# Expert stage 1 of a two-block transformer kernel: gate steps of four tokens, gates stored in pairs, and a lookup by predicated copies

## The chip, the cores and the metric

The kernel runs on one core of one Trainium2 chip. The metric is the device time of one execution in microseconds (us), as the median of several runs. A core has five engines that work side by side, each through its own queue in order: TensorE (PE; PEld is its weight load), VectorE (DVE), ScalarE (ACT), GpSimd (POOL) and SyncE (SP), which issues most of the DMAs. TensorE writes to PSUM, a small memory of eight banks; VectorE and ScalarE can read PSUM, GpSimd cannot.

## The reference

One attention block with a product-key expert layer (PEER), then a second block of two mixers. The change is in the expert layer, for 512 tokens of width 1024, eight heads and 16384 = 128 x 128 experts:

```python
q = (hx @ w_q).reshape(TOKEN_BLOCK, PEER_HEADS, 2, PEER_HALF)
s = einsum('nhpd,hpkd->nhpk', q, sub_keys)               # 2 x 128 scores a head
top_s, top_i = lax.top_k(s, PEER_TOPK)                   # 16 of each half
cand = top_s[:, :, 0, :, None] + top_s[:, :, 1, None, :]
best_s, best_p = lax.top_k(cand.reshape(..., 256), PEER_TOPK)
i1 = take_along_axis(top_i[:, :, 0], best_p // PEER_TOPK)
i2 = take_along_axis(top_i[:, :, 1], best_p % PEER_TOPK)
expert = i1 * N_KEYS + i2                                # 8 x 16 experts a token
gate = softmax(best_s)
act = gelu(einsum('nd,ned->ne', hx, u[expert]))
return einsum('ne,ned->nd', gate * act, v[expert])
```

## The kernel before

The 512 tokens are four tiles of 128. Tile 0 gathers its experts' rows of `u` and `v` from memory and takes row dots (`gathered`, L713). For tiles 1 to 3 (384 tokens) the layer is computed over all experts, in 128 blocks of 128 experts: activations of every token with every expert, times a gate matrix that is zero where a token did not choose an expert.

Expert stage 1 is the loop at L731 over the first SPILL = 88 blocks. A block (`experts_in`, L694) loads 512 KB of `u`, splits it into a high part on ScalarE (L690) and a low part on GpSimd (L691), multiplies it with the tokens in 24 matmuls into one PSUM buffer of the tag `acc` (four buffers), and takes the gelu on ScalarE into `av` (L703), which a DMA stores in A_d (L736). Stage 2 (L803) does the other 40 blocks with `experts_out`, reads back A_d and the gates, multiplies them (L754), and adds up the output.

Between the blocks of stage 1 a hand-made plan (L679 to L685) places other work. A plan entry has a block number; all entries that are due are emitted ahead of that block.

`route(t)` finds the experts of tile t in five steps, spread over ROUTE_AT[t]. Each of the first four does four heads of one half: four or eight matmuls of the queries q2T with the sub-keys skT into a PSUM buffer of the tag `lg` (two buffers; L570), then max, index and replace on VectorE (L576 to L580). q2T[0] holds heads 0 to 3 (steps one and two), q2T[1] the others (steps three and four). The fifth step sums candidates (`cand`, L584, L587), picks 16 of them (L595 to L599), and looks up which key each stands for: the place in the list is split by shifts into two numbers (L602 to L615), and for each half a one-hot compare over 16 places (L624), a product with the indices (L627) and a tree of adds (L629, L630) give `ii`. Then the softmax of the gates.

`slot_major(t)` transposes `ii` and the gates into `eT` through a PSUM buffer of the tag `tp` (two buffers). `gate_matrix(g)` makes the gates of 16 tokens in four steps of four tokens in a row: VectorE compares `eT` with 0..127 for both halves at once into `oh` (L661), ScalarE scales the second half by the gate (L666), TensorE multiplies the two one-hots into a `tp` buffer (L667), and ScalarE writes the four 128 x 128 results into `stage` (L668), which a DMA stores in G_d (L669). `stage` and q2T have the tag "stage" and share its two buffers (L553, L657). GATES_AT places these entries.

The instructions of an engine are not run in the order of the text: the framework orders them by a list schedule with the text's order as priority, and gives a tile its buffer when one is free. Only the transfers marked so keep the order of the text.

Of the kernel before, what the change touches and what calls it, by code (L numbers as in the profile page):

```python
# [10 lines left out]
FT = mybir.dt.float32  # L11
# [12 lines left out]
OT = 8  # L24
# [6 lines left out]
ROUTE_AT = ((0, 12), (12, 25), (25, 44), (44, 63))  # L31
GATES_AT = ((27, 49), (49, 67), (67, 85))
# [59 lines left out]
def block_kernel(ctx: ExitStack, tc: tile.TileContext, A, out):  # L92
# [428 lines left out]
    for j in range(2):  # L521
# [11 lines left out]
    G_d = dram.tile([HG, P, P, GT], FT, name="G_d")  # L533
# [24 lines left out]
    NC1, NC2 = 4 * TOPK, (TOPK - 4) * 4  # L558
    NCD = NC1 + NC2

    def route(t, found):
# [21 lines left out]
        cand = rw.tile([P, PH, NCD], FT, name="cand")  # L583
# [3 lines left out]
        nc.vector.tensor_add(cand[:, :, NC1:NCD].rearrange("p h (a b) -> p h a b", b=4),  # L587
# [21 lines left out]
        late = rw.tile([P, NSLOT], BF, name="late")
        nc.vector.tensor_scalar(late, df[:, 0], 4.0, None, op0=OP.is_ge)  # L610
        abf = rw.tile([P, 2, NSLOT], BF, name="abf")
        nc.vector.scalar_tensor_tensor(df[:, 2], df[:, 2], -12.0, df[:, 0], op0=OP.add, op1=OP.subtract)
        nc.vector.tensor_sub(df[:, 3], df[:, 3], df[:, 1])
        nc.vector.tensor_mul(df[:, 2:4], df[:, 2:4], late[:, None, :].to_broadcast([P, 2, NSLOT]))
        nc.vector.tensor_add(abf, df[:, 0:2], df[:, 2:4])  # L615
        ii = rw.tile([P, 2, NSLOT], FT, name="ii")
        for hf in range(2):
            eq = rw.tile([P, TOPK, NSLOT], BF, name="eq", tag="oh", bufs=4)
            eqs = eq.rearrange("p j (g s) -> p j g s", s=OT)

            tif = rw.tile([P, TOPK, PH, TOPK], BF, name="tif")
            nc.scalar.activation(tif, ti[:, hf].rearrange("p h j -> p j h")[:, :, :, None]
                                 .to_broadcast([P, TOPK, PH, TOPK]), AF.Copy)
            nc.vector.tensor_tensor(eqs, iota_t[:, :, None, :].to_broadcast([P, TOPK, NSLOT // OT, OT]),  # L624
                                    abf[:, hf].rearrange("p (g s) -> p g s", s=OT)[:, None]
                                    .to_broadcast([P, TOPK, NSLOT // OT, OT]), op=OP.is_equal)
            nc.vector.tensor_mul(eq, eq, tif.rearrange("p j h s -> p j (h s)"))  # L627
            for n in (8, 4, 2):
                nc.vector.tensor_add(eq[:, 0:n], eq[:, 0:n], eq[:, n:2 * n])  # L629
            nc.vector.tensor_add(ii[:, hf], eq[:, 0], eq[:, 1])  # L630
# [12 lines left out]
    eT = rz.tile([P, 3, TG], FT, name="eT")  # L643
    found = {}

    def slot_major(t):
# [6 lines left out]
        nc.scalar.activation(eT[:, :, (t - 1) * P:t * P], p[:, 0:3], AF.Copy)  # L653

    def gate_matrix(g):

        stage = rz.tile([P, P, GT], FT, name="stage", tag="stage", bufs=2)  # L657
        for t0 in range(0, GT, 4):
            c = slice(g * GT + t0, g * GT + t0 + 4)
            oh = rw.tile([P, 2, 4, P], FT, name="oh", tag="oh", bufs=4)  # L660
            nc.vector.tensor_tensor(oh, iota_f[:, None, None, :].to_broadcast([P, 2, 4, P]),  # L661
                                    eT[:, 0:2, c, None].to_broadcast([P, 2, 4, P]), op=OP.is_equal)
            p = ps.tile([P, 4, P], FT, name="tp", tag="tp")
            for i in range(4):
                at = g * GT + t0 + i
# [532 lines left out]
```

## Time and profile before

| what | us |
|---|---|
| median of three runs | 2403.86 (2402.47 to 2408.37) |
| the profiled execution, of which the rows are | 2402.58 |
| its span in the trace | 2400.8 |
| TensorE busy in the span | 2255.2 (94%) |
| VectorE, ScalarE, GpSimd busy | 1695.4, 1138.6, 1073.5 |
| expert stage 1, from the first block's split to the second stage's first outputs | about 406 to 985 |

A row of a view names a line of the kernel, the engine, the operation, and which tile is made from which. Busy time is what an engine worked; the idle time in front of an instruction is put down to what ended it. The granted clock (PEclk) is 1.00 at 2.4 GHz and 0.50 at 1.2 GHz; a number between is a mean over a stretch.

### The profile page before, as it was taken

How to read it: one execution, taken by the hardware profiler on the slowest of the kernel's cores; microseconds unless marked ns; L12 is line 12 of the kernel's file. 1: busy time of each engine (PE TensorE's matmuls, PEld its weight loads, DVE VectorE, ACT ScalarE, POOL GpSimd, SP SyncE). 2: the span in 40 equal slices, each digit the busy share in tenths (PEclk: the TensorE clock that was granted, in tenths of full speed). 3: DMA queues.
4: the chain of work that ended last, by engine and by line, in shares of the span. 5: the costliest groups of instructions: out<-in, count | busy, mean ns of one | idle time of the engine just before them, and what ended most of it. 6: DMA issues, size and time to landing. Idle time of an engine off the chain costs nothing.

```text
span 2400.8 us, 32593 instructions
## 1 busy us (share of the span) xinstructions
PE 2255.2 (94%) x11610; PEld 1930.8 (80%) x11610; DVE 1695.4 (71%) x2982; ACT 1138.6 (47%) x2093; POOL 1073.5 (45%) x643
## 2 busy tenths in 40 slices
PE   6989999996998989899999999999899899999998
PEld 5767778996988889799998788888788788867676
DVE  8698445499778777588888888888655445247755
ACT  3644423433467979533333333333455444367742
POOL 4840034565755654388876665656211302212200
PEclk9999999998999999999999999999999999999999
DMA  7456123465766676799998999998311222312121
GB/s 273 143 183 189 62 80 106 150 211 179 246 225 239 242 249 230 262 346 339 333 332 312 341 339 324 327 337 303 116 36 36 71 100 63 112 40 65 32 74 67
DMA packets 205570, 463.04 MB, mean 193 GB/s; under 512 B 17664, under 2 KB 98016, under 8 KB 202336
## 3 DMA queue, kind: packets, MB, share of 16 engines
q1 hardware_dynamic: 168544, 326.72, 41.1%
q0 software_dynamic: 36864, 134.23, 15.3%
q8 instruction: 92, 1.51, 0.3%
q14 instruction: 70, 0.57, 0.1%
HBM read 415.26 MB, written 44.58 MB: 192 GB/s over the span
## 4 chain that ended last, share of the span: by engine, by line
PE 64%; DVE 16%; issue 7%; DMA 6%; ACT 5%; POOL 3%; SPq 0%; DVEq 0%; POOLq 0%; ACTq 0%
PE acc L153 14%; PE acc L154 14%; PE acc L155 14%; PE lg L153 2%; PE lg L154 2%; PE lg L155 2%; PE tp L154 2%; PE tp L153 2%; PE tp L155 2%; PE lg L1095 2%; DMA g<-in_peer_u_dram,idx 2%; DVE oh L661 1%; PE tp L667 1%; DVE g L717 1%; DVE wada L267 1%
## 5 line engine op out<-in xcount | busy, mean ns | idle before, releaser
L691 POOL TENSOR_TENSOR wlo<-wraw,whi 128x1024 fp32r<-128x1024 f32 x172 | 453.8, 2640 | 430.7 <-ACT whi L690 424.4
L690 ACT ACTIVATE whi<-wraw 128x1024 fp32r<-128x1024 f32 x256 | 269.1, 1053 | 221.1 <-PE lg L154 61.4
L153 PE MATMUL acc<-fm,whi 128*128 128x384 f32 (+2 forms) x932 | 329.0, 355 | 7.0 <-ACT av L703 5.1
L154 PE MATMUL acc<-fm,whi 128*128 128x384 f32 (+2 forms) x932 | 323.3, 348 | 0.0
L155 PE MATMUL acc<-fm,wlo 128*128 128x384 f32 (+2 forms) x932 | 321.6, 347 | 1.3 <-POOL wlo L691 1.3
L717 DVE CUSTOM_DVE_ANT_0 g<-g,h20y 128x1024 f32<-128x1024 f32 x128 | 199.0, 1559 | 85.6 <-DMA g<-in_peer_u_dram,idx 85.2
L149 POOL TENSOR_TENSOR wlo<-wraw,whi 128x1024 fp32r<-128x1024 f32 (+4 forms) x56 | 124.4, 2232 | 288.4 <-ACT whi L148 283.5
L757 ACT ACTIVATE wh<-w 128x384 fp32r<-128x384 f32 x128 | 67.0, 524 | 331.9 <-DVE w L754 277.3
L148 ACT ACTIVATE whi<-wraw 128x1024 fp32r<-128x1024 f32 (+5 forms) x142 | 138.1, 980 | 158.6 <-PE acc L155 83.4
L154 PE MATMUL acc<-wlo,wh 128*128 128x512 f32 x512 | 203.0, 397 | 5.1 <-POOL wlo L691 5.0
L728 DVE SCALAR_TENSOR_TENSOR h20y<-g,act,h20y 128x1024 f32<-128x1024 f32 x127 | 189.7, 1494 | 20.3 <-DMA g<-in_peer_v_dram,idx 19.9
L155 PE MATMUL acc<-whi,wl 128*128 128x512 f32 x512 | 201.8, 395 | 0.4 <-DVE wl L758 0.4
L153 PE MATMUL acc<-whi,fm 128*128 128x512 f32 (+3 forms) x496 | 189.7, 387 | 3.6 <-ACT fm L139 2.4
L153 PEld LDWEIGHTS acc<-fm,whi 128*128 128x128 f32 x932 | 176.9, 191 | 19.0 <-ACT av L703 5.4
L709 POOL DMA_INDIRECT g<-in_peer_u_dram,idx x128 | 178.3, 1393 | 29.8 <-issue 16.4
L155 PE MATMUL acc<-whi,fm 128*128 128x512 f32 (+3 forms) x496 | 188.0, 385 | 0.0
L154 PE MATMUL acc<-wlo,fm 128*128 128x512 f32 (+3 forms) x496 | 187.9, 381 | 0.0
L154 PEld LDWEIGHTS acc<-fm,whi 128*128 128x128 f32 x932 | 177.3, 190 | 9.5 <-issue 2.2
L155 PEld LDWEIGHTS acc<-fm,wlo 128*128 128x128 f32 x932 | 177.0, 190 | 9.0 <-POOL wlo L691 1.8
L709 POOL DMA_INDIRECT g<-in_peer_v_dram,idx x128 | 167.2, 1307 | 33.9 <-issue 19.6
L153 PE MATMUL acc<-whi,wh 128*128 128x512 f32 x512 | 182.1, 395 | 0.0
L149 DVE TENSOR_TENSOR wlo<-wraw,whi 128x1024 fp32r<-128x1024 f32 (+3 forms) x86 | 102.3, 1196 | 88.3 <-ACT whi L148 84.6
(356 smaller groups left out, 5415.1 us busy)
## 6 DMA issues: line engine op xcount, KB each, us to landing
wraw<-in_uT_dram SPq DMA_DIRECT2D x128, 512.0 KB
wraw<-in_peer_v_dram SPq DMA_DIRECT2D x128, 512.0 KB
wada<-in_w_adaT_dram SPq DMA_DIRECT2D x48, 512.0 KB
G_d<-stage SPq DMA_DIRECT2D x24, 1024.0 KB
gm<-G_d SPq DMA_DIRECT2D x64, 384.0 KB
A_d<-av SPq DMA_DIRECT2D x88, 192.0 KB
am<-A_d SPq DMA_DIRECT2D x88, 192.0 KB
wraw<-in_w_in_dram SPq DMA_DIRECT2D x24, 512.0 KB
```

Source lines behind the costliest of these rows:

```text
L148: nc.scalar.activation(hi[:, :nk, :n], raw[:, :nk, :n], AF.Copy)
L149: eng.tensor_sub(lo[:, :nk, :n], raw[:, :nk, :n], hi[:, :nk, :n].bitcast(FT))
L153: nc.tensor.matmul(o, lh, rh, start=first, stop=False)
L154: nc.tensor.matmul(o, lh, rl, start=False, stop=False)
L155: nc.tensor.matmul(o, ll, rh, start=False, stop=last)
L690: nc.scalar.activation(hi, raw, AF.Copy)
L691: eng.tensor_sub(lo, raw, hi.bitcast(FT))
L709: tc.keep_in_program_order(nc.gpsimd.indirect_dma_start(out=g, out_offset=None, in_=src, in_offset=bass.IndirectOffsetOnAxis(ap=idx0[:, s: ...
L717: nc.vector.tensor_tensor_reduce(out=g, in0=g, in1=h20, scale=1.0, scalar=0.0, op0=OP.mult, op1=OP.add, accum_out=act0[:, i:i + 1])
L728: nc.vector.scalar_tensor_tensor(y, g, act0[:, s:s + 1], y, op0=OP.mult, op1=OP.add)
L757: nc.scalar.activation(wh, w, AF.Copy)
L1095: nc.tensor.matmul(lg, q[:, t * P:(t + 1) * P], k, start=True, stop=True)
```

## The change

- The gates of a tile are planned in 32 steps of four tokens, one entry each, where there were eight of 16 tokens; a step's result goes into a PSUM buffer of the tag `acc` and no longer `tp`.
- `eT` is not copied to SBUF: the compares read the transposed indices from the `tp` buffer in PSUM. Only the gates are copied (`gT`).
- `stage` and G_d hold pairs of neighbouring key numbers beside each other, [64, 16 tokens, 2] for [128, 16 tokens]; the reader in stage 2 takes every second element.
- The one-hot lookup is replaced by a binary one: the place is cut into four bits, and predicated copies halve a list of 16 until one is left. ScalarE fills the first list and copies the result.
- `cand` has 16 more places between its parts, filled with the lowest number by GpSimd in every route, so that a place splits by bits alone.
- The sub-keys are stored twice, each time with zeros in the other half's rows, and L570 multiplies over 128 rows.
- ROUTE_AT and GATES_AT are moved a little, and tile 0's 60 row dots of this stage are spread over blocks 24 to 87 instead of 13 to 87.

```diff
-ROUTE_AT = ((0, 12), (12, 25), (25, 44), (44, 63))
-GATES_AT = ((27, 49), (49, 67), (67, 85))
+ROUTE_AT = ((0, 11), (11, 23), (23, 43), (43, 62))
+GATES_AT = ((24, 45), (45, 65), (65, 85))
...
-    skT = rz.tile([P, PH, N_KEYS], FT, name="skT")
-    dma(skT, A["subkeysT"])
+    skT = rz.tile([P, PH, 2, N_KEYS], FT, name="skT")
+    for a in range(2):
+        own, other = slice(a * 64, (a + 1) * 64), slice((1 - a) * 64, (2 - a) * 64)
+        nc.gpsimd.memset(skT[other, :, a], 0.0)
+        dma(skT[own, :, a], A["subkeysT"][own])
...
-                    nc.tensor.matmul(lg[:, h * P:(h + 1) * P], q2T[h0 // 4][b0:b0 + 64, h, t * P:(t + 1) * P],
-                                     skT[b0:b0 + 64, h0 + h], start=True, stop=True)
+                    nc.tensor.matmul(lg[:, h * P:(h + 1) * P], q2T[h0 // 4][:, h, t * P:(t + 1) * P],
+                                     skT[:, h0 + h, hf], start=True, stop=True)
...
+        nc.gpsimd.memset(cand[:, :, NC1:NC2], MARK)
...
+        nc.vector.tensor_scalar(ab[:, 0], bpf, 4, 3, **shift_and)
+        nc.vector.tensor_scalar(ab[:, 1], bpf, 15, None, op0=OP.bitwise_and)
+        nc.vector.tensor_scalar(late[:, 0], bpf, 2, 15, **shift_and)
+        nc.vector.tensor_scalar(late[:, 1], bpf, 3, None, op0=OP.bitwise_and)
+        nc.vector.tensor_scalar(far, bpf, 64, None, op0=OP.bitwise_and)
+        nc.vector.copy_predicated(ab, far[:, None, :].to_broadcast([P, 2, NSLOT]), late)
+        bits = rw.tile([P, 4, 2, NSLOT], U32, name="bits")
+        for n in range(4):
+            nc.vector.tensor_scalar(bits[:, n], ab, 1 << n, None, op0=OP.bitwise_and)
...
+            eq = rw.tile([P, 8, NSLOT], FT, name="eq", tag="oh", bufs=4)
+            eqh = eq.rearrange("p j (h s) -> p j h s", h=PH)
+            nc.scalar.activation(eqh, tif[:, hf, 0:8, :, None].to_broadcast([P, 8, PH, TOPK]), AF.Copy)
+            nc.vector.copy_predicated(eqh, bits[:, 3, hf]...,  tif[:, hf, 8:16, :, None]...)
+            for n in (4, 2, 1):
+                nc.vector.copy_predicated(eq[:, 0:n], bits[:, n.bit_length() - 1, hf]..., eq[:, n:2 * n])
+            nc.scalar.activation(ii[:, hf], eq[:, 0], AF.Copy)
...
-        nc.scalar.activation(eT[:, :, (t - 1) * P:t * P], p[:, 0:3], AF.Copy)
+        nc.scalar.activation(gT[:, (t - 1) * P:t * P], p[:, 2], AF.Copy)
+        eT[t - 1] = p[:, 0:2]
...
+    def gate_matrix(q):
+        g, t0 = q * 4 // GT, q * 4 % GT
+        if t0 == 0:
+            stages[g] = rz.tile([P, P // 2, GT, 2], FT, name="stage", tag="stage", bufs=2)
+        e = eT[q * 4 // P][:, :, q * 4 % P:q * 4 % P + 4, None]
+        oh = rw.tile([P, 2, 4, P], FT, name="oh", tag="oh", bufs=4)
+        nc.vector.tensor_tensor(oh, iota_f[:, None, None, :].to_broadcast([P, 2, 4, P]),
+                                e.to_broadcast([P, 2, 4, P]), op=OP.is_equal)
+        p = ps.tile([P, 4, P], FT, name="gp", tag="acc", bufs=4)
+        for i in range(4):
+            nc.scalar.activation(oh[:, 1, i], oh[:, 1, i], AF.Copy, scale=gT[:, q * 4 + i:q * 4 + i + 1])
+            nc.tensor.matmul(p[:, i], oh[:, 0, i], oh[:, 1, i], start=True, stop=True)
+        nc.scalar.activation(stages[g][:, :, t0:t0 + 4], p.rearrange("p i (u w) -> p u i w", w=2), AF.Copy)
+        if t0 + 4 == GT:
+            dma(G_d[g], stages.pop(g))
...
-    turn, first_turn = 0, int(ROUTE_AT[0][1]) + 1
+    turn, first_turn = 0, int(ROUTE_AT[1][1]) + 1
```

## Rows read from the trace of the kernel before

**Rows 1.** The page's slices of 60 us: TensorE busy in tenths.
```profile
PE   6989999996998989899999999999899899999998
```
**Rows 2.** Stage 1 in stretches: length, busy us (instructions) of each engine, clock, DMA.
```profile
core 0: us, PE busy (x) PEld busy (x) DVE busy (x) ACT busy (x) POOL busy (x), PEclk, DMA share, GB/s
...
550.00:600.00 50.00, 33.09 (x174) 31.88 (x175) 48.89 (x111) 22.47 (x45) 27.73 (x14) 0.80 0.53 178
...
700.00:750.00 50.00, 42.04 (x257) 40.39 (x256) 38.45 (x84) 33.62 (x63) 25.19 (x12) 0.93 0.61 217
750.00:800.00 50.00, 43.62 (x278) 42.66 (x279) 47.46 (x114) 42.95 (x93) 30.74 (x13) 0.97 0.63 215
800.00:850.00 50.00, 48.40 (x319) 47.01 (x319) 35.74 (x33) 44.52 (x91) 29.89 (x14) 1.00 0.75 265
850.00:900.00 50.00, 43.68 (x271) 42.18 (x270) 36.48 (x33) 38.10 (x83) 30.02 (x14) 0.97 0.71 243
...
950.00:985.00 35.00, 22.30 (x144) 20.40 (x143) 19.13 (x20) 30.46 (x68) 6.22 (x4) 0.90 0.62 236
sum 579.00, PE 518.22 PEld 498.84 DVE 432.47 ACT 360.85 POOL 321.44; mean PE 43.18 PEld 41.57 DVE 36.04 ACT 30.07 POOL 26.79
```
**Rows 3.** Waits of TensorE, 406 to 990: us in total, times, longest.
```profile
PE tp L667 <- ACT stage L668: 20.0, 19, 2.5
PE tp L650 <- DVE ii L630: 15.5, 1, 15.5
PE tp L667 <- ACT oh L666: 10.4, 4, 5.2
PE lg L153 <- ACT am L703: 5.6, 1, 5.6
PE acc L153 <- ACT av L703: 5.1, 1, 5.1
```
**Rows 4.** Timeline, TensorE and ScalarE: start us, us, engine, instruction.
```profile
587.30 0.27 PE L667 MATMUL tp<-oh 128*128 128x128 f32 x1
...
665.85 1.16 PE L570 MATMUL lg<-skT,q2T 64*128 64x128 f32 x8
...
667.16 1.07 ACT L668 ACTIVATE stage<-tp 128x512 f32<-128x512 f32 x1
```
**Rows 5.** Timeline, VectorE: first and last operation of one route step.
```profile
445.21 0.30 DVE L576 MAX8 ts<-lg 128x8 f32<-128x128 f32 x1 [38.56 <-PE lg L570]
...
450.04 0.28 DVE L580 FIND_INDEX8 ti<-ts,s 128x8 uint32<-128x128 f32 x1
```
**Rows 6.** VectorE on `eq`, on `df` (busy, count); two adds, 406 to 990 (busy, mean).
```profile
406.00:990.00 584.00, 51.46 (x48) 0.96 0.65 218
...
406.00:990.00 584.00, 14.69 (x24) 0.96 0.65 218
...
L629 DVE TENSOR_TENSOR eq<-eq 128x256 bf16<-128x256 bf16 x8 | 14.4, 1797 | 0.0
...
L629 DVE TENSOR_TENSOR eq<-eq 128x1024 bf16<-128x1024 bf16 x8 | 6.9, 863 | 0.0
```
**Rows 7.** VectorE's compare (also min/median/max ns) and row dots, 406 to 990.
```profile
L661 DVE TENSOR_TENSOR oh<-iota_f,eT 128x1024 f32<-128x1024 f32 x96 | 140.4, 1501 | 11.3 <-ACT stage L668 9.6 <-PE tp L667 1.3 <-ACT oh L666 0.3
...
L661 DVE TENSOR_TENSOR oh<-iota_f,eT x96: 1199/1218/3434, 581.1 to 972.3; 128x1024 f32<-128x1024 f32 x96
...
L717 DVE CUSTOM_DVE_ANT_0 g<-g,h20y 128x1024 f32<-128x1024 f32 x63 | 104.9, 1666 | 61.4 <-DMA g<-in_peer_u_dram,idx 61.1 <-issue 0.4
```
**Rows 8.** ScalarE from PSUM, 512 elements: into `stage`, and in runs.
```profile
L668 ACT ACTIVATE stage<-tp 128x512 f32<-128x512 f32 x96 | 94.9, 1069 | 7.9 <-DMA G_d<-stage 6.2 <-PE tp L667 1.7
...
L139 ACT ACTIVATE fm<-tp 128x512 fp32r<-128x512 f32 x48 | 27.3, 595 | 49.8 <-PE tp L137 49.7
```
**Rows 9.** VectorE's max over PSUM and over SBUF, 406 to 990.
```profile
L576 DVE MAX8 ts<-lg 128x8 f32<-128x128 f32 x56 | 16.3, 290 | 49.3 <-PE lg L570 49.3
...
L579 DVE MAX8 ts<-s 128x8 f32<-128x128 f32 x56 | 15.6, 278 | 0.0
```
**Rows 10.** The product with `gm` in stage 2: min/median/max ns.
```profile
L754 DVE TENSOR_TENSOR w<-am,gm x128: 543/552/3284, 992.2 to 1669.3; 128x384 f32<-128x384 f32 x128
```

More of the change, by code (lines that the diff above doesn't have):

```diff
@@ L532, in block_kernel @@
     HG = TG // GT
-    G_d = dram.tile([HG, P, P, GT], FT, name="G_d")
+    G_d = dram.tile([HG, P, P // 2, GT, 2], FT, name="G_d")
     A_d = dram.tile([P, P, TG], FT, name="A_d")
@@ L556, in block_kernel @@
     linear_fm(A["w_peer_q"][0], 8, 512, 512, h2T, NT, lambda m, p: nc.scalar.activation(q2T[1][:, m], p, AF.Copy))
-    NC1, NC2 = 4 * TOPK, (TOPK - 4) * 4
-    NCD = NC1 + NC2
+    NC1, NC2, NCD = 4 * TOPK, 5 * TOPK, 8 * TOPK
+    cand = rz.tile([P, PH, NCD], FT, name="cand")
     def route(t, found):
@@ L609, in route @@
[L609 to L615, printed above, removed]
+        ab = rw.tile([P, 2, NSLOT], U32, name="ab")
@@ new lines, in route @@
+        late = rw.tile([P, 2, NSLOT], U32, name="late")
+        far = rw.tile([P, NSLOT], U32, name="far")
+        shift_and = dict(op0=OP.logical_shift_right, op1=OP.bitwise_and)
+        nc.vector.tensor_scalar(ab[:, 0], bpf, 4, 3, **shift_and)
[3 more added lines that the diff above has]
+        nc.vector.tensor_scalar(far, bpf, 64, None, op0=OP.bitwise_and)
@@ L616, in route @@
+        nc.vector.copy_predicated(ab, far[:, None, :].to_broadcast([P, 2, NSLOT]), late)
+        bits = rw.tile([P, 4, 2, NSLOT], U32, name="bits")
+        for n in range(4):
+            nc.vector.tensor_scalar(bits[:, n], ab, 1 << n, None, op0=OP.bitwise_and)
+        tif = rw.tile([P, 2, TOPK, PH], FT, name="tif")
+        nc.scalar.activation(tif, ti.rearrange("p f h j -> p f j h"), AF.Copy)
         ii = rw.tile([P, 2, NSLOT], FT, name="ii")
         for hf in range(2):
-            eq = rw.tile([P, TOPK, NSLOT], BF, name="eq", tag="oh", bufs=4)
@@ L627, in route @@
[L627 to L630, printed above, removed]
+            eq = rw.tile([P, 8, NSLOT], FT, name="eq", tag="oh", bufs=4)
+            eqh = eq.rearrange("p j (h s) -> p j h s", h=PH)
+            nc.scalar.activation(eqh, tif[:, hf, 0:8, :, None].to_broadcast([P, 8, PH, TOPK]), AF.Copy)
+            nc.vector.copy_predicated(eqh, bits[:, 3, hf].rearrange("p (h s) -> p h s", h=PH)[:, None]
+                                      .to_broadcast([P, 8, PH, TOPK]),
+                                      tif[:, hf, 8:16, :, None].to_broadcast([P, 8, PH, TOPK]))
@@ L631, in route @@
+            for n in (4, 2, 1):
+                nc.vector.copy_predicated(eq[:, 0:n], bits[:, n.bit_length() - 1, hf][:, None]
+                                          .to_broadcast([P, n, NSLOT]), eq[:, n:2 * n])
+            nc.scalar.activation(ii[:, hf], eq[:, 0], AF.Copy)
         ge = rw.tile([P, PH, TOPK], FT, name="ge")
@@ L640, in route @@
         yield
-    eT = rz.tile([P, 3, TG], FT, name="eT")
+    eT = {}
+    gT = rz.tile([P, TG], FT, name="gT")
     found = {}
@@ L652, in slot_major @@
         nc.tensor.transpose(p[:, 2], gt, ident)
-        nc.scalar.activation(eT[:, :, (t - 1) * P:t * P], p[:, 0:3], AF.Copy)
[L655 to L665, printed above, removed]
-                nc.scalar.activation(oh[:, 1, i], oh[:, 1, i], AF.Copy, scale=eT[:, 2, at:at + 1])
-                nc.tensor.matmul(p[:, i], oh[:, 0, i], oh[:, 1, i], start=True, stop=True)
-            nc.scalar.activation(stage[:, :, t0:t0 + 4].rearrange("p i t -> p t i"), p, AF.Copy)
-        dma(G_d[g], stage)
+        nc.scalar.activation(gT[:, (t - 1) * P:t * P], p[:, 2], AF.Copy)
+        eT[t - 1] = p[:, 0:2]
+    stages = {}
+    def gate_matrix(q):
[13 more added lines that the diff above has]
+            dma(G_d[g], stages.pop(g))
     def first_indices():
@@ L683, in block_kernel @@
         plan.append((a, lambda t=t: slot_major(t)))
-        plan += [(at, lambda g=g: gate_matrix(g)) for g, at in enumerate(spread(P // GT, a, b), (t - 1) * P // GT)]
+        plan += [(at, lambda q=q: gate_matrix(q)) for q, at in enumerate(spread(P // 4, a, b), (t - 1) * P // 4)]
     plan.sort(key=lambda step: step[0])
@@ L778, in fetch_gates @@
             if part == 0:
-                gts[b] = dz.tile([P, HG, 8, GT], FT, name="gm")
+                gts[b] = dz.tile([P, HG, 4, GT, 2], FT, name="gm")
             c = slice(part * HG // 4, (part + 1) * HG // 4)
-            paced(gts[b][:, c], G_d[c, :, b:b + 8].rearrange("g p i t -> p g i t"))
+            paced(gts[b][:, c], G_d[c, :, b // 2:b // 2 + 4].rearrange("g p u t w -> p g u t w"))
     def fetch(n):
```

24 lines of the change are left out of this document (2 added, 22 removed).

## The prediction

> **What bounds the kernel now.** I read the page's slices of 60 us first [rows 1]: TensorE is busy nearly everywhere. What the change touches, expert stage 1, lies in slices 7 to 17, and there stand a 6 in slice 10 and an 8 in 13, 15 and 17. So I asked for that stage in 50 us stretches [rows 2]. It runs from about 406 to 985 us. Over these 579 us TensorE was busy 518.2, so 60.8 us were idle; and the granted clock fell to 0.80, 0.93, 0.97, 0.97 and 0.90 in five stretches, which is 0.20 x 50 + 0.07 x 50 + 0.03 x 50 + 0.03 x 50 + 0.10 x 35 = 20.0 us of full-speed time. TensorE's matmuls of the stage are not altered by the diff, so 60.8 + 20.0 = 80.8 us is all that it can win there.
>
> Then the waits of TensorE in the stage [rows 3]. Two kinds stand out. The first is VectorE falling behind: a single wait of 15.5 us for the looked-up indices `ii` of tile 1 and one of 5.1 us for an accumulator that ScalarE could not empty; VectorE was busy 48.9 of the 50 us around them [rows 2], and the clock fell to 0.80 in the same stretch. The second is the gate matrices: 20.0 us waiting for ScalarE's evacuation into `stage` and 10.4 us for its scaling of `oh`, in 23 pieces, because four steps of four tokens are emitted in a row behind one plan entry, while only two PSUM buffers of the tag `tp` take their results. The 5.6 us at the end belong to the tail, where the last gate steps have no expert block left beside them.
>
> One more thing must be seen, for it decides the forecast [rows 4]. The gate steps of tile 1 are planned from block 27, and their first matmuls do run at 587.30 us. But the first evacuation starts at 667.16 us, 80 us later, right behind the eight matmuls of L570 at 665.85. These are the second step of route(3), the last readers of q2T[0]. q2T and `stage` share the tag "stage" with two buffers: no gate tile can be written until route(3) has read q2T[0]. In those 80 us two finished gate results sat in the two `tp` buffers. That cost TensorE nothing, since the experts use the tag `acc`.
>
> **The change, part by part.**
>
> Lookups. What touches `eq` and `df`, the one-hot lookup and the arithmetic on its indices, took 51.5 + 14.7 = 66 us of VectorE over four tiles [rows 6]. The 256-element add in it took 1797 ns, twice the 1024-element one (863), so what makes these operations long is being held up, not their size. New are, per tile, nine predicated copies (one over 256, and for each half 1024, 512, 256, 128 elements) and nine short bit operations in place of five. No predicated copy is in this trace. From below I scale the shortest compare, 1199 ns for 1024 elements [rows 7]: (256 + 2 x 1920) / 1024 x 1.2 = 4.8 us, rounded up to 5.5 for the fixed part of the short ones, and 2.5 for the bit operations: 8 us a tile. From above each copy is held as that 256-element add was, about 1.5 us more: 22 us a tile. I take 12, nearer the lower end since fewer operations wait on each other; that saves 66 - 48 = 18 us of VectorE (bounds: 34 saved, 22 lost). ScalarE loses eight 2048-wide broadcasts and gains eight 1024-wide ones and some small copies, even.
> By the Trainium skill, "SBUF — State Buffer", section "Who interferes with whom", a VectorE instruction with two SBUF inputs contends with a GpSimd instruction that reads SBUF. By it the predicated copies, with list and bits both in SBUF, are exposed like the adds, which agrees with the 1797 ns [rows 6]; with every one held the lookups would cost 22 us more than now in place of 18 less, and VectorE would be late again where it was late for `ii`.
>
> Indices out of PSUM. 96 compares of 1501 ns mean, 140.4 us, with a median of 1218 and a longest of 3434 [rows 7]. The second operand moves from SBUF to PSUM. The nearest rows are the max over `lg` (PSUM), 290 ns, and over `s2` (SBUF), 278 ns [rows 9]: 12 ns more, 1.2 us over 96. If the hold-ups go as well, up to 0.28 x 96 = 27 us fall away. I take 15 us of VectorE saved, bounds 1 lost and 27 saved.
>
> Pairs. The evacuation takes 1069 ns for 512 elements that it writes 64 bytes apart [rows 8]; the same size written in runs takes 595 ns. Now eight elements lie together, but PSUM is read two by two. No row shows such a read: bounds 0.60 and 1.07 us; I take 0.7, near the run-wise row, 96 x 0.37 = 35 us of ScalarE. Behind it, the product with `gm` reads every second element; its shortest runs take 543 ns for 384 elements [rows 10]. Doubled, it would add 0.4 us x 128 to VectorE in stage 2; I take nothing, and keep 10 us of loss in the range.
>
> Four-token steps. 96 steps spread singly over blocks 24 to 85: a step's scalings and evacuation on ScalarE now lie beside a block of experts instead of beside three other steps. That should take most of the 20.0 + 10.4 us of waits, and the tail's 5.6, since the last step is planned at block 84. The stretch 800:850, where gates already alternate with blocks, shows what is left: 1.6 us idle in 50 at full clock [rows 2].
>
> Padded sub-keys: the same 128 columns per matmul, nothing on TensorE; one more DMA and two GpSimd fills before the stage, four fills of `cand` in it (128 elements a partition each), and candidates 128 wide instead of 112: about 3 us of VectorE in all. GpSimd is busy 321 of 579 us [rows 2], so its fills hide; were they not hidden they would cost some 5 us.
>
> Row dots from block 24 instead of 13: the same 60 of 1666 ns [rows 7], so tiles 0 and 1 are routed without them, which takes some ten dots, 17 us, out of the stretch in which VectorE was full. In exchange 0.95 instead of 0.82 of them per block later. I let the 15.5 and 5.1 us waits go for that and the lighter lookups.
>
> What is late next: the gate results now take the tag `acc`, four buffers, which the experts need too. Each holds its buffer until its evacuation, and that waits for q2T[0] as in [rows 4]. From block 24 four results can be ready within some four blocks; then all four buffers are held, and behind them in TensorE's order every expert block waits. TensorE is then free for nothing but the `lg` matmuls of the routes, so routes 2 and 3 are pulled forward until q2T[0] is read. With two `lg` buffers that takes three steps of route(2) on VectorE. One step takes 445.21 to 450.32, 5.1 us [rows 5]. So 3 x 5.1 = 15.3, plus four compares of 1.2 and some five dots of 1.2 (their length when not held up, as the compare's) that come before them, 4.8 + 6: 26 us of hold. For the second `stage` buffer (q2T[1]) one more short hold, 4 us, between nothing and one step.
>
> The sum: 80.8 us of loss now, against 26 + 4 of holds, 10 of clock (what the stretch with the 16.9 idle us lost) and 13 of ordinary waits (1.6 in 50 over the 410 us behind block 24): 53. Gain 28. Stage 2 follows unchanged: the gathers left to it are the same. The profiled execution took 2402.58 us (span 2400.8), 1.3 below the median of 2403.86, against which I set it: 2403.9 - 28 = 2376.
>
> **The rivals.**
> No hold: the buffers of `acc` go to the experts first, and gates trail as they did in `tp`. For it: in [rows 4] gates waited 80 us while experts ran. Against: there the two had different tags. Loss left: 13 and 3 of clock; gain 65: 2339 us.
> Hold as long as the gain: 50 us instead of 26, since the small VectorE operations are held up as in [rows 6]; with 15 of clock and 13 of waits the loss is near the old one: 2403. The skill's rule named above speaks for this one, as far as GpSimd still has blocks to split during the hold.
> Slower: q2T[0] is freed only when route(3) comes in its planned turn, block 47, and VectorE first does everything before it: three steps of route(2), 15, its lookups and sorting, 19, two steps of route(3), 10, and some 22 dots of 1.67, 37: 81 us of hold, 20 of clock, 13 of waits, 114 against 80.8: 2437 us. It turns slower as soon as the holds are over some 50 us.
> The change not doing what it says: pairs without effect on the evacuation. ScalarE then keeps its 35 us, of the 218 that it is idle in the stage (579 - 360.9, [rows 2]), and some of the waits on it stay; a sixth of the 30.4 us is 5: 2381, inside the forecast's own range.
>
> **How the numbers follow.** About 0.3%, 7 us, can be told from no change. Forecast 0.44 (its own range 2358 to 2394, from a hold of 12 to 42 us), no hold 0.25, even 0.13, slower 0.18. So faster by over 0.3%: 0.69; within: 0.13; slower: 0.18. The range for 8 in 10 runs from 2337 (no hold) to 2416 (all but the heavier part of the slow case, with the 10 us of the strided product).
>
> **What would show it.** Right: evacuations at some 0.7 us; compares near 1.22 us; no 15 us wait for `ii`; around 550 us one stretch in which TensorE waits for ScalarE's evacuation, with the `lg` matmuls of routes 2 and 3 inside it; the stage's end near 957 us. Wrong: evacuations that start soon behind the first gate matmul, or experts that run while gate results wait (no hold); or `lg` matmuls of route(3) still at their old distance with TensorE idle before them (slower).

## The result, and the profile after

The changed kernel takes 2365.5 us, median of four runs (2365.3 to 2372.3), against 2404.0 us for the kernel before in the same series: 38 us or 1.6% less, ratio 0.984, 95% interval [0.983, 0.985]. The forecast was 2376 us in a range of 2337 to 2416: faster, as said, by some 10 us more than said. The profiled execution has a span of 2363.3 us against 2400.8.

First, where the 37.5 us of span lie. Two rows of ScalarE bracket stage 1: its first and last `av` are the gelus of expert blocks 0 and 87, and the last `am` is that of the last expert block in stage 2. The first row of each pair is stage 1, of before and of after (count; min/median/max ns; first and last start, us).

```profile
L703 ACT ACTIVATE av<-acc x88: 458/473/519, 429.4 to 949.2; 128x384 f32<-128x384 f32 x88
L703 ACT ACTIVATE am<-lg x40: 468/472/493, 983.8 to 1301.5; 128x384 f32<-128x384 f32 x40
```
```profile
L706 ACT ACTIVATE av<-acc x88: 463/472/491, 432.6 to 944.6; 128x384 f32<-128x384 f32 x88
L706 ACT ACTIVATE am<-lg x40: 468/472/491, 949.5 to 1267.0; 128x384 f32<-128x384 f32 x40
```

At the last `am` the changed kernel is 34.5 us ahead; at the first `av` it was 3.2 us behind. So stage 1 and its change to stage 2 bring 37.7 us; the 3.2 us lost ahead of them and the 3.0 won behind the last `am` cancel. And not evenly: block 87 comes only 4.6 us earlier, the first `am` 34.3 us. What went is the stretch from 949 to 984 us, in which the kernel before had no block of stage 1 left and worked off gate steps.

The stage in stretches, after; columns as in [rows 2]:

```profile
core 0: us, PE busy (x) PEld busy (x) DVE busy (x) ACT busy (x) POOL busy (x), PEclk, DMA share, GB/s
...
500.00:550.00 50.00, 37.43 (x214) 36.84 (x213) 41.52 (x174) 21.68 (x39) 23.38 (x11) 0.85 0.48 157
550.00:600.00 50.00, 36.48 (x212) 35.38 (x212) 46.41 (x231) 21.01 (x47) 13.56 (x9) 0.81 0.30 103
...
650.00:700.00 50.00, 41.88 (x269) 40.71 (x269) 34.57 (x36) 28.36 (x70) 27.33 (x15) 0.96 0.79 276
...
900.00:949.00 49.00, 49.00 (x310) 49.00 (x309) 18.21 (x22) 25.16 (x52) 20.16 (x12) 1.00 0.87 289
sum 543.00, PE 504.73 PEld 496.98 DVE 362.41 ACT 321.91 POOL 292.68; mean PE 45.88 PEld 45.18 DVE 32.95 ACT 29.26 POOL 26.61
```

Idle time of TensorE fell from 60.8 to 543 - 504.7 = 38.3 us. From 600 us on TensorE is nearly full, but for 8.1 us idle between 650 and 700, and the end of the stage is clean (49.00 of 49.00, where [rows 2] has 22.30 of 35). Most of what is left sits between 500 and 600 us, and there it is worse than before: 26.1 us idle in these 100 us, where the kernel before had 21.9 (33.09 of 50 busy in [rows 2], and before it this row):

```profile
500.00:550.00 50.00, 45.06 (x260) 43.09 (x258) 48.48 (x159) 13.80 (x19) 36.57 (x19) 1.00 0.72 239
```

The waits of TensorE, 400 to 1000 us, after (total, times, longest), which answer to [rows 3]:

```profile
PE gp L669 <- ACT oh L668: 12.6, 3, 6.5
PE lg L570 <- DVE s L578: 11.3, 2, 8.2
PE tp L649 <- ACT ii L628: 9.0, 1, 9.0
PE gp L669 <- ACT av L706: 3.1, 3, 1.5
PE acc L152 <- ACT stage L670: 2.2, 2, 1.6
```

The 20.0 us for the evacuation are down to 2.2, the 5.6 us of the tail and the 5.1 us for the accumulator are gone. The 15.5 us for `ii` became 9.0. The 10.4 us for `oh` did not fall: they are 12.6, in three waits. New are 11.3 us in which a route's `lg` matmuls wait for VectorE. The operations themselves (count | busy us, mean ns):

```profile
L664 DVE TENSOR_TENSOR oh<-iota_f,tp 128x1024 f32<-128x1024 f32 x96 | 113.8, 1212 | 27.4 <-ACT whi L693 22.6 <-PE gp L669 3.8 <-ACT ii L628 0.5
...
L670 ACT ACTIVATE stage<-gp 128x512 f32<-128x512 f32 x96 | 54.6, 590 | 6.8 <-DMA G_d<-stage 3.5 <-PE gp L669 3.0 <-PE lg L570 0.3
...
L622 DVE COPY_PREDICATED eq<-bits,tif 128x1024 f32<-128x1024 uint32 x8 | 10.4, 1341 | 0.0
L613 DVE TENSOR_SCALAR bits<-ab 128x256 uint32<-128x256 uint32 x16 | 9.8, 669 | 0.0
L626 DVE COPY_PREDICATED eq<-bits,eq 128x512 f32<-128x512 uint32 x8 | 9.5, 1225 | 0.0
```

And the hold that the forecast was built on, TensorE's and ScalarE's instructions of the gates and the routes from the first gate matmul on (start us, us):

```profile
546.61 0.80 PE L669 MATMUL gp<-oh 128*128 128x128 f32 x2 [3.62 <-ACT oh L668]
...
560.34 1.95 PE L570 MATMUL lg<-skT,q2T 128*128 128x128 f32 x16
...
562.12 1.06 PE L669 MATMUL gp<-oh 128*128 128x128 f32 x8
571.37 2.08 PE L570 MATMUL lg<-skT,q2T 128*128 128x128 f32 x8 [8.19 <-DVE s L578]
576.56 2.08 PE L570 MATMUL lg<-skT,q2T 128*128 128x128 f32 x8 [3.12 <-DVE s L578]
...
578.67 2.07 ACT L670 ACTIVATE stage<-gp 128x512 f32<-128x512 f32 x4 [0.30 <-PE lg L570]
```

Four gate results, the last at 562.12; then TensorE does nothing but `lg` matmuls of routes 2 and 3, which wait for VectorE; at 576.56 the second step of route 3 reads q2T[0] for the last time; at 578.67 four evacuations run in a row. In [rows 4] the first evacuation came at 667.16, 80 us behind the first gate matmul; here it is 32 us.

### The profile page after: what moved, and what is told of

The parts are those of the page before. It is cut to its first block, busy times and chain, and to the rows that moved or that the text cites. A ratio compares the mean times of both kernels' runs of the same rounds, so it can differ in the third digit from the quotient of the medians.

```text
span 2363.3 us, 32554 instructions
## 1 busy us (share of the span) xinstructions
PE 2240.4 (95%) x11610; PEld 1929.5 (82%) x11610; DVE 1631.9 (69%) x2966; ACT 1100.5 (47%) x2105; POOL 1045.0 (44%) x648
## 3 DMA queue, kind: packets, MB, share of 16 engines
q0 software_dynamic: 36864, 134.23, 15.5%
## 4 chain that ended last, share of the span: by engine, by line
PE 69%; DVE 12%; DMA 7%; issue 6%; ACT 3%; POOL 3%; SPq 0%; DVEq 0%; POOLq 0%; ACTq 0%
PE acc L152 15%; PE acc L154 15%; PE acc L153 15%; PE gp L669 3%; PE lg L153 2%; PE lg L152 2%; PE lg L154 2%; PE tp L153 2%; PE tp L154 2%; PE tp L152 2%; PE lg L1098 2%; DMA wraw<-in_peer_v_dram 2%; DMA g<-in_peer_u_dram,idx 2%; DVE wada L266 1%; PE tp L136 1%
## 5 line engine op out<-in xcount | busy, mean ns | idle before, releaser
L694 POOL TENSOR_TENSOR wlo<-wraw,whi 128x1024 fp32r<-128x1024 f32 x172 | 444.3, 2584 | 419.9 <-ACT whi L693 418.7
L720 DVE CUSTOM_DVE_ANT_0 g<-g,h20y 128x1024 f32<-128x1024 f32 x128 | 187.1, 1465 | 108.0 <-DMA g<-in_peer_u_dram,idx 107.4
L712 POOL DMA_INDIRECT g<-in_peer_v_dram,idx x128 | 162.1, 1267 | 34.6 <-issue 19.4
L712 POOL DMA_INDIRECT g<-in_peer_u_dram,idx x128 | 162.4, 1269 | 26.0 <-issue 14.7
## 6 DMA issues: line engine op xcount, KB each, us to landing
wraw<-in_uT_dram SPq DMA_DIRECT2D x128, 512.0 KB
wraw<-in_peer_v_dram SPq DMA_DIRECT2D x128, 512.0 KB
wada<-in_w_adaT_dram SPq DMA_DIRECT2D x48, 512.0 KB
wraw<-in_w_in_dram SPq DMA_DIRECT2D x24, 512.0 KB
```

What stands on the lines that cost most here:

```text
L694: eng.tensor_sub(lo, raw, hi.bitcast(FT))
L712: tc.keep_in_program_order(nc.gpsimd.indirect_dma_start(out=g, out_offset=None, in_=src, in_offset=bass.IndirectOffsetOnAxis(ap=idx0[:, s: ...
L720: nc.vector.tensor_tensor_reduce(out=g, in0=g, in1=h20, scale=1.0, scalar=0.0, op0=OP.mult, op1=OP.add, accum_out=act0[:, i:i + 1])
```

## The experiments

Each kernel's ratio is to runs of the kernel before on the same chip. Beside it stands the stage by the first and last `av` of its profiled execution, since the start of the stage alone moves by some 4 us between kernels that differ in nothing ahead of it. The kernel before has 429.4 to 949.2 there, 519.8 us, with gate steps to 979 behind it.

| kernel | median, us | ratio to before, 95% | first to last `av`, us |
|---|---|---|---|
| changed | 2365.5 | 0.9838 [0.9825, 0.9852] | 432.6 to 944.6: 512.0 |
| changed, again (control) | 2365.6 | 0.9848 [0.9826, 0.9871] | 432.4 to 941.4: 509.0 |
| pairs undone | 2379.4 | 0.9868 [0.9836, 0.9899] | 435.6 to 956.6: 521.0 |
| single steps undone | 2380.8 | 0.9885 [0.9857, 0.9914] | 434.8 to 963.2: 528.4 |
| dots from block 12 | 2380.6 | 0.9878 [0.9849, 0.9907] | 436.1 to 957.2: 521.1 |
| lookups undone | 2376.8 | 0.9893 [0.9871, 0.9914] | 433.8 to 953.2: 519.4 |
| compares from SBUF | 2388.6 | 0.9942 [0.9920, 0.9965] | 436.7 to 965.1: 528.4 |
| gates in `tp` | 2441.3 | 1.0130 [1.0101, 1.0159] | 435.0 to 875.9, gates to 1021 |
| before, single steps alone | 2408.6 | 1.0009 [0.9998, 1.0021] | 434.5 to 955.8, gates to 986 |
| before, gates in `acc` alone | 2410.7 | 1.0025 [1.0014, 1.0036] | 433.1 to 994.0: 560.9 |
| gates and dots later | 2356.9 | 0.9803 [0.9786, 0.9819] | 435.3 to 934.2: 498.9 |
| q2T[0] read early | 2342.9 | 0.9740 [0.9711, 0.9768] | 432.7 to 922.6: 489.9 |
| q2T[0] read early, dots later | 2347.8 | 0.9775 [0.9758, 0.9791] | 433.3 to 923.3: 490.0 |

> The changed kernel itself, unaltered, beside the others on this chip: 0.984 of the kernel before, with the waits of TensorE that its first trace shows (9.0 us for `ii`, 11.3 on `lg` for VectorE, 12.6 for `oh`).

It came out so, with waits of 9.0, 10.6 and 11.9 us. The two series of the changed kernel differ by 0.001 in the ratio and by 3 us in the stage; below, "slower by" is given by the ratio and by the stage, against the mean of the two (0.9843 and 510.5 us). The intervals reach some 0.003 to either side, so by the ratio alone "pairs undone" can't be told from the changed kernel, and "single steps undone" and "dots from block 12" hardly; the stage parts them more clearly, but by one profiled execution each.

**The hold: gate results out of `acc`.**

```diff
-        p = ps.tile([P, 4, P], FT, name="gp", tag="acc", bufs=4)
+        p = ps.tile([P, 4, P], FT, name="gp", tag="tp")
```

> The changed kernel with the gate results back in the PSUM tag `tp` (of whose two buffers the indices of the tile hold one), so that a gate result that waits for `stage` holds no buffer that experts need. Theory: the stretch from 546 to 579 us in which four results sit in `acc` costs TensorE 11 us of waiting for the routes' `lg` plus 3 to 7 of clock: without it 8 to 15 us are won, less what a single buffer costs later in waits of one gate matmul for the evacuation before it (96 steps, up to 0.2 us each, 19): 2352 to 2370 us, and no wait of TensorE on `lg` for VectorE over 3 us. Rival: the hold costs nothing of its own, VectorE being behind in any case: the single buffer alone shows, 2370 to 2390, and the same 11 us of waiting stand at another place.

Measured 2441 us, outside both. The first half of the theory shows: no wait of TensorE on `lg` is left, and the experts run on; block 40 comes at 618.8 us (671.9 in the changed kernel) and the last at 875.9. But the gate steps stay behind. Nothing forces the routes forward, so the first evacuation is at 642 us and the last at 1021. Evacuations of this kernel (first and last start), and its stretches at the end:

```profile
L670 ACT ACTIVATE stage<-gp x96: 572/597/600, 642.3 to 1021.4; 128x512 f32<-128x512 f32 x96
```
```profile
900.00:950.00 50.00, 36.57 (x150) 32.21 (x151) 27.41 (x27) 35.36 (x97) 0.00 (x0) 0.53 0.21 84
950.00:1000.00 50.00, 37.63 (x148) 32.34 (x147) 21.98 (x18) 34.07 (x92) 0.00 (x0) 0.50 0.26 105
```

For 100 us TensorE has little but gate matmuls, four tokens at a time behind one buffer, at a granted clock of 0.53 and 0.50; its waits for the evacuation sum up to 46.9 us from 400 to 1000 us, 24.0 of them in these 100. So the hold in `acc` is a price with a return: TensorE stands, and thereby the routes come and the gate steps stay beside the experts. How much of the loss goes to the late start and how much to the single buffer, this run does not part.

**The same switch on the kernel before**, results in `acc` alone (bursts, layout, lookups and dots as before).

> The kernel before with the gate results in `acc` instead of `tp` alone, all else as before. Theory: the experts now wait behind held results, so the route steps that read q2T[0] are pulled forward and the first evacuation comes by some 620 us instead of 667; the gate steps end with the experts and the tail goes, but the hold costs TensorE some 20 to 30 us: within 12 us of before, 0.995 to 1.005 of it. Rival: the hold is a pure loss: 15 us or more slower, over 1.006, with the gate steps no earlier.

The theory's time held: 1.0025. Waits, the places of two of them, and evacuations:

```profile
PE lg L570 <- DVE s L578: 34.4, 3, 25.9
PE gp L667 <- ACT av L703: 18.0, 15, 5.8
```
```profile
577.09 2.08 PE L570 MATMUL lg<-skT,q2T 64*128 64x128 f32 x8 [25.93 <-DVE s L578]
...
584.20 5.22 PE L667 MATMUL gp<-oh 128*128 128x128 f32 x24 [4.20 <-ACT oh L666]
```
```profile
L668 ACT ACTIVATE stage<-gp x96: 1025/1080/1147, 604.3 to 969.7; 128x512 f32<-128x512 f32 x96
```

First evacuation at 604 us instead of 667, and the tail is gone; new waits eat all of it. They are not the hold of the forecast, though one of them is as long: the 25.9 us, from 551 to 577, lie ahead of the first gate matmul at 584, when no gate result exists yet. There the third step of route 2 stands in TensorE's queue ahead of the transposes of tile 1 and the next expert block, and waits for VectorE; the kernel before waited 15.5 us for `ii` at that place. With gate results held, TensorE waits only 8.5 us on `lg` (5.4 and 3.1). The other new cost is 18.0 us in which gate matmuls wait for an `acc` buffer that a gelu has not emptied.

**Single four-token steps alone on the kernel before.**

```diff
-        plan += [(at, lambda g=g: gate_matrix(g)) for g, at in enumerate(spread(P // GT, a, b), (t - 1) * P // GT)]
+        plan += [(at, lambda q=q: gate_matrix(q)) for q, at in enumerate(spread(P // 4, a, b), (t - 1) * P // 4)]
```

> The kernel before with single four-token gate steps alone: one plan entry for each, spread over the old blocks 27 to 85, results still in `tp`, all else as before. Theory: the waits in bursts (20.0 us for the evacuation, 10.4 for `oh`) are cut, but the first evacuation stays near 667 us, since q2T[0] is read in its planned turn and the experts don't wait for a gate result in `tp`; so the gate steps still run late and into a tail: 5 to 15 us faster than before, 0.994 to 0.998 of it. Rival: the single steps are the main part of the change: 20 us or more faster, under 0.992.

1.0009: nothing, a miss of mine. Its waits:

```profile
PE tp L670 <- ACT stage L671: 16.0, 17, 2.0
PE tp L650 <- DVE ii L630: 15.5, 1, 15.5
PE tp L670 <- ACT oh L669: 14.1, 7, 5.2
```

The bursts are still there: 30.1 us where [rows 3] has 30.4. The first evacuation is at 671.9 us, after 48 of the 88 gelus, and by then nearly all of tile 1's steps, planned over blocks 27 to 48, are due; a backlog comes in a row however finely it was planned.

**The same edit undone in the changed kernel**: four steps in a row behind one entry.

> The changed kernel with four four-token steps emitted in a row again, one plan entry for 16 tokens at the entry's old spacing, all else as changed. Theory: the single steps carry most of the gain: the waits of TensorE for the evacuation and for `oh` come back, 15 to 30 us slower, 2380 to 2395 us. Rival: those waits came of the slow evacuation, and the priority order in TensorE's queue mixes bursts with experts anyway: within 6 us of the changed kernel, 2360 to 2372.

Slower by 10 us (ratio) or 18 us (stage): the theory's price, near its lower end, but not its mechanism. The waits for the evacuation and for `oh` did not come back; those for `ii` grew (9.0 to 24.1, while `oh` fell from 12.6 to 5.2):

```profile
PE tp L649 <- ACT ii L628: 24.1, 3, 8.9
...
PE gp L669 <- ACT oh L668: 5.2, 3, 3.6
```

The two new waits, 8.8 and 6.3 us, are at the changes to tiles 2 and 3, whose transposes come behind 40 and 60 gelus here and behind 44 and 64 in the changed kernel; why they come earlier stays open. With evacuations from 574 us on there is no backlog. The edit is worth nothing in the kernel before, and 10 to 18 us beside the other changes.

**Pairs undone** (`stage`, G_d and `gm` as before).

```diff
-        nc.scalar.activation(stages[g][:, :, t0:t0 + 4], p.rearrange("p i (u w) -> p u i w", w=2), AF.Copy)
+        nc.scalar.activation(stages[g][:, :, t0:t0 + 4].rearrange("p i t -> p t i"), p, AF.Copy)
```

> The changed kernel with the layout of before for `stage`, G_d and `gm`, all else as changed. The evacuation goes back from 590 to some 1070 ns, 96 x 0.48 = 46 us more of ScalarE. Theory: a gate step lies beside an expert block and ScalarE was idle over a third of the stage, so most of this hides: at most 8 us slower than the changed kernel, 2365 to 2373 us. Rival: ScalarE feeds the gate steps and the pairs carry the gain: 20 us or more slower, over 2385.

```profile
L670 ACT ACTIVATE stage<-gp 128x512 f32<-128x512 f32 x96 | 97.4, 1084 | 8.7 <-DMA G_d<-stage 4.5 <-PE gp L669 3.9 <-PE lg L570 0.3
```

43 us of ScalarE are back (97.4 - 54.6), 6 to 10 us of them show: near the theory's upper end of 8. In plain time, 2379 us lies between both ranges; on this chip the kernel before took 2409. The product with `gm` takes 548 ns in the median here, 550 in the changed kernel: reading every second element costs nothing.

**Row dots from block 12 again.**

```diff
-    turn, first_turn = 0, int(ROUTE_AT[1][1]) + 1
+    turn, first_turn = 0, int(ROUTE_AT[0][1]) + 1
```

> The changed kernel with the row dots from block 12 again, all else as changed. Theory of the prediction: VectorE gets about ten dots more between 500 and 600 us, where it is what TensorE waits for: 5 to 15 us slower, 2370 to 2380 us. Rival: what holds VectorE is not the dots' own 1.2 us but waits of its queue for late gathers (6.3 us at 558 and 6.5 us at 690 in the changed kernel), and these are as many with an early start or fewer: the same or up to 10 us faster, 2355 to 2366.

8 to 11 us slower, the theory's side. TensorE's waits on `lg` for VectorE go from 11.3 to 29.5 us, most of it in one:

```profile
561.32 2.08 PE L570 MATMUL lg<-skT,q2T 128*128 128x128 f32 x8 [24.59 <-DVE s L578]
```

It stands ahead of the transposes of tile 1 (563 us), where the changed kernel waits 9.0 us for `ii`, and no wait for `ii` is left. So `lg` and `ii` together went from 20.3 to 29.5; with gate results held, the wait is 4.9 us, less than the 11.3 of the changed kernel. That VectorE also waits for late gathers is true, but an early start does not mend it.

**Lookups of before.**

> The changed kernel with the one-hot lookup of before (indices shifted for the padded candidates), all else as changed. VectorE's lookups take some 66 us instead of 47. Theory: tile 1's lookup is what TensorE waits for at 533 us, and tile 2's and 3's steps end the hold: 5 to 10 us of the extra 19 show, 2370 to 2378 us. Rival: the lookups are covered: within 3 us of the changed kernel.

9 to 12 us slower, the theory's side and a little over. The wait on `lg` is 22.4 us, 11 more, but the 9.0 us for `ii` are gone here too:

```profile
549.57 2.07 PE L574 MATMUL lg<-skT,q2T 128*128 128x128 f32 x8 [15.22 <-DVE s L582]
```

This wait, ahead of the transposes of tile 1 at 551.6 us, is 6 us longer than the one for `ii` in its place, so tile 1's lookup shows as the theory said. The other half of the theory does not: with gate results held, the wait is 7.2 us, not more than 11.3. TensorE's waits for `oh` are 16.1 us for 12.6; the rest of the loss is spread.

**Compares from SBUF**: the transposed indices copied out of PSUM first.

```diff
-        eT[t - 1] = p[:, 0:2]
+        eS = rz.tile([P, 2, P], FT, name="eS")
+        nc.scalar.activation(eS, p[:, 0:2], AF.Copy)
+        eT[t - 1] = eS
```

> The changed kernel with the transposed indices copied to SBUF (one buffer) and compared from there, all else as changed. Theory: the compares go from 1.21 back to some 1.5 us, 28 us of VectorE over 96 steps, nearly all at places where VectorE has time: 0 to 6 us slower, 2365 to 2371. Rival: the compare is the head of each gate step's chain, and its length shows: 10 us or more slower, over 2375.

18 to 24 us slower, the rival's side: by the ratio the dearest undoing, by the stage level with the single steps. Rows of this kernel: the compare on VectorE, then GpSimd's split and gather issues from 450 to 950 us (count | busy us, mean ns), then the compare's min/median/max here and, last, in the changed kernel.

```profile
L666 DVE TENSOR_TENSOR oh<-iota_f,eS 128x1024 f32<-128x1024 f32 x96 | 152.6, 1616 | 6.6 <-PE gp L671 3.1 <-ACT oh L670 1.6 <-ACT whi L695 1.1
```
```profile
L696 POOL TENSOR_TENSOR wlo<-wraw,whi 128x1024 fp32r<-128x1024 f32 x81 | 217.6, 2687 | 185.4 <-ACT whi L695 183.5 <-PE lg L570 1.5
L714 POOL DMA_INDIRECT g<-in_peer_u_dram,idx x60 | 87.0, 1451 | 9.0 <-issue 3.3 <-PE gp L671 0.2
```
```profile
L666 DVE TENSOR_TENSOR oh<-iota_f,eS x96: 1164/1216/3433, 549.4 to 940.2; 128x1024 f32<-128x1024 f32 x96
```
```profile
L664 DVE TENSOR_TENSOR oh<-iota_f,tp x96: 1161/1214/1231, 544.9 to 915.5; 128x1024 f32<-128x1024 f32 x96
```

The median is equal, 1216 and 1214 ns; the longest is 3433 against 1231. What a PSUM operand takes away is the hold-ups alone, and all of them: not one compare in 96 is over 1231 ns. The other side gains too: the split takes 2687 ns here and 2555 in the changed kernel, a gather's issue 1451 and 1098, the row dots 1617 and 1443. ScalarE's waits for a compare are 98.6 us here and 54.1 there, and TensorE's waits for `oh`, and of gate matmuls for an `acc` buffer that a gelu has not emptied, 17.0 + 8.6 against 12.6 + 3.1. One confound stays: the copy has one buffer, so the next tile's transposes wait for the last compare of this one.

**Gates and dots later** (gates from block 27, dots from block 30, routes where they were).

> The changed kernel with the gates from block 27 and the row dots from block 30 alone, as in the version with q2T[0] read early, but with the route steps at their own places. Theory: q2T[0] is still read only when TensorE stands behind held gate results, so a wait of 8 us or more on `lg` for VectorE stays: at most 8 us faster than the changed kernel, 2357 to 2368 us. Rival: the 20 us that the early version won came of the later gates and dots: 2340 to 2350 us.

2356.9 us, 10 to 12 us faster than the changed kernel, a little more than the theory's 8: the 9.0 us wait for `ii` is gone, the hold stays:

```profile
PE gp L669 <- ACT oh L668: 17.0, 4, 7.3
PE lg L570 <- DVE s L578: 9.0, 2, 7.9
```

**q2T[0] read early**: in addition, the first two steps of routes 2 and 3 ahead of the first gate step, and their later steps some blocks earlier too.

```diff
-ROUTE_AT = ((0, 11), (11, 23), (23, 43), (43, 62))
-GATES_AT = ((24, 45), (45, 65), (65, 85))
+STEPS_AT = ((0, 2.2, 4.4, 6.6, 8.8), (11, 13.2, 15.4, 17.6, 19.8), (22, 23.5, 29, 32, 35), (25, 26.5, 40, 44, 48))
+GATES_AT = ((27, 47), (47, 66), (66, 85))
...
-    turn, first_turn = 0, int(ROUTE_AT[1][1]) + 1
+    turn, first_turn = 0, 30
```

> The changed kernel with other due times alone: the two steps of routes 2 and 3 that read q2T[0] come before the first gate step (planned at blocks 22 to 26.5, the gates from 27), the later steps of these routes at blocks 29 to 48, the row dots from block 30. So q2T[0] is free when the first gate results want `stage`. Theory: the waits of TensorE between 525 and 600 us (24 us idle in the changed kernel, and a clock of 0.85 and 0.81) come of the hold; without it 12 to 25 us faster than the changed kernel, 2340 to 2353 us, evacuations right behind the first gate matmuls. Rival: VectorE is what is late there, in whatever order its steps stand: TensorE waits as long on `lg` or `ii` at another place, 2360 to 2372 us.

2342.9 us, 21 to 25 us faster than the changed kernel and 2.6% faster than the kernel before; 9 to 15 us of it beyond the version with later gates alone. Waits, and three stretches:

```profile
PE gp L670 <- ACT oh L669: 17.5, 8, 8.3
PE lg L571 <- DVE s L579: 2.5, 1, 2.5
```
```profile
550.00:600.00 50.00, 48.12 (x323) 47.93 (x322) 41.06 (x145) 35.47 (x84) 27.87 (x15) 1.00 0.62 214
600.00:650.00 50.00, 42.69 (x252) 41.30 (x251) 50.00 (x144) 33.63 (x80) 27.39 (x16) 0.93 0.71 244
650.00:700.00 50.00, 41.16 (x252) 40.40 (x251) 48.94 (x131) 31.16 (x68) 24.69 (x15) 0.90 0.70 246
```

The first evacuation starts at 557.8 us, 4.3 behind the first gate matmul instead of 32, and TensorE keeps full clock to 600 us. It did not have to stand for the routes to come: they only had to be planned ahead. What is left moved to 600 to 700 us, where VectorE is full.

**The same, with the dots from block 45** and the late route steps spread wider.

> The version with q2T[0] read early, with VectorE relieved between 600 and 700 us: the last three steps of route 2 at blocks 29, 33, 37, of route 3 at 43, 50, 57, the row dots from block 45 instead of 30. Theory: what is left of its loss is VectorE full from 600 to 700 us (waits of TensorE for `oh`, 17.5 us, 8.3 of them at 682 us, and the clock at 0.93 and 0.90): 8 to 15 us faster than that version, 2327 to 2336 us. Rival: the dots, now 60 in 42 blocks, make VectorE or GpSimd late behind block 45: no faster, 2340 us or more.

2347.8 us, the rival's side: no faster (stage 490.0 us against 489.9). From 600 to 650 us TensorE gains 6.6 us of busy time, and between 700 and 800 us it loses 7.9, where dots and gathers are now denser.

## Why the prediction was right, point by point

**The bound and the place** were right: all of the gain is in stage 1, and the waits of the tail and for the evacuation went. Those for `oh` did not (10.4 before, 12.6 after): 3.6 us are the first `oh` behind the late `ii`, 6.5 a late row dot (below).

**The hold** happened as told, by its signs too: four results in `acc`, route steps pulled forward, evacuations right behind L570. Its size was off: 26 + 4 us forecast, 11.3 us of waiting on `lg` measured, and the second hold, of 4 us, did not come at all. The step that failed is "three steps of route(2)" plus dots within the hold. The first two steps of route 2 had run before it, at 527 and 532 us, ahead of TensorE's wait for `ii`; VectorE worked on them during that wait and beside the blocks behind it, which ran on until 560, so two steps were left for the hold. Nor does any other run show the forecast's size: with results held in `acc`, TensorE waited 4.9 to 13.3 us on `lg` in the five undoings and 8.5 in the kernel before with `acc` alone.

**"I let the 15.5 and 5.1 us waits go"** was half wrong. 9.0 us for `ii` of tile 1 stayed and 3.6 us for the first `oh` behind it. The lookup got shorter, but the gate steps were put three blocks earlier in the plan and the route's last step only two, and I did not set the one against the other.

**Ordinary waits** were taken from a stretch without tile changes, and missed one that the row dots bring. The chain of waits of the changed kernel, around the change to tile 2:

```profile
688.99 7.40 DMA g<-in_peer_u_dram,idx
...
697.65 1.15 DVE oh L664
...
698.82 0.41 ACT oh L668
...
699.27 0.80 PE gp L669 x2
```

VectorE's queue has a row dot at its head whose gathered row is not there; the compares of the next gate steps stand behind it, and TensorE is idle for 6.5 us (692.8 to 699.3). The 6.3 us at 558 us that I named in the expectation of "dots from block 12" are no such wait: so long a gather's transfer is in the chain there, but VectorE stood idle for it only 1.3 us.

**The sum** had a mistake of method. I added the clock's loss to the idle time, 60.8 + 20.0, but the windows' clock counts the idle time too. Laid over the gaps between TensorE's matmuls, the clock of the two traces lost 9.1 us before and 11.6 after in idle time, and 11.5 and 10.5 in busy time. So the clock gave back about 1 us, where the sum has 10. What fell is idle time (22.5) and, counted from each matmul's start to the next one's, gaps left out, gate matmuls (90.8 to 82.7), expert blocks (383.4 to 380.3), routes (16.2 to 14.6) and stage 2, with which the kernel before had begun in its tail (9.9 to 5.5); against them, 3.7 us more lie ahead of the first block and in the transposes. That makes the 36 us between the stretches of 579 and 543 us. With the clock left out and the hold as measured the sum would read 60.8 - 11.3 - 13 = 36.5 us of gain, near the 38 measured, though only since two omissions cancel: 12.6 us of waits for `ii` and the first `oh` that stayed, and 13.5 us less of busy time. So that the measured gain lies as near the forecast as it does is in part luck.

**The single costs.** Lookups: 12 us a tile forecast, 47.0 us in four tiles measured (`eq` 28.0, `bits` 9.8, the rest 9.2). That some predicated copies would be held up came true in part: those of 512 elements took 706 to 2727 ns, the eight of 1024 elements 1271 to 1369. Evacuation: 0.7 forecast, 0.59 measured, just under the lower bound. Product with `gm`: nothing, as taken. Compares: 1.22 forecast, 1.212 measured, 26.6 us saved, the top of the bounds; but their worth was mis-sized, since I saw them as covered time of VectorE. They are the head of each gate step's chain and delay GpSimd as well, and undoing them costs 18 to 24 us.

**The parts do not add up**: the five undoings cost 66 us by the stage's length, the whole change brings 38. They do not share it by lengthening one hold: with results held, the waits on `lg` stay at 4.9 to 13.3 us against 11.3. What grew is the wait ahead of the first gates (dots, lookups), the waits for `ii` at later tiles (single steps) and many short ones (pairs, compares); in all five the clock's loss in busy time grew too, from 10.5 to between 11.5 and 15.2 us. How the 38 us divide is open.

**The rivals.** "No hold" fell by the timeline. "Even" comes to 2401 us by its own terms (50 + 15 + 13 = 78 of 80.8), not 2403, which changes nothing. "Slower" needed routes that come only in their planned turn; they were pulled forward. The kernel with gates in `tp` shows that a still slower case existed that I had not priced: no hold, and gates that never catch up.

## What to carry to other kernels

When a result waits for a buffer that another stage still reads, ask which queue it stops: if it stops nothing, its work silently gathers into a tail; if it stops the main engine, that engine's idleness pulls the missing reader forward; best is to plan the last reader ahead of the first writer, which here, with later gates, added more than half of what the whole change had brought. Count idle time and the clock's loss on busy time, never the clock over a window with gaps. An edit of the plan is worth only what the first thing that blocks it lets through, so try it with that block gone. And before a long wait is put down to a cause, look where it stands: the 25.9 us on `lg` had the length of the forecast hold, but lay ahead of it.

## What the runs showed of the hardware

A compare with one operand in PSUM was never held up beside GpSimd's work (1161 to 1231 ns over 96), the same compare with both in SBUF up to 3433 ns, and GpSimd's split and gather issues grew with it, by 5% and 32%. The Trainium skill, "SBUF — State Buffer", section "Who interferes with whom", says that a VectorE instruction with at most one SBUF input, outside the two-port modes, does not contend with GpSimd, and that one with two SBUF inputs contends with a GpSimd instruction that reads SBUF. The traces agree on both sides. That the short bit operations on one SBUF input took up to 2496 ns (median 282) fits the exception. No view shows which mode they ran in; the medians of such an operation, 216 ns for 128 elements and 282 for 256, make 0.5 ns an element more, an estimate, where the compare's 1214 ns for 1024 are 1.2 each. Reading PSUM two elements at a time cost nothing: 590 ns for 512 elements against 595 in runs [rows 8]; with the old layout it is 1084 again, so what had cost was writing 64 bytes apart.
